# First input projection of a two-layer backbone: fed from x times the scale alone, with the reciprocal root applied where it leaves PSUM

## The chip, the core and the metric

The kernel runs on one core of one Trainium2 chip, in one launch. The metric is device time in microseconds (us), from the first to the last instruction of the core and what lies around them. TensorE is called PE, its weight loads PEld, VectorE DVE, ScalarE ACT, GpSimd POOL; SP is the engine that issues the transfers.

## The reference

Two layers work on 512 latent tokens (`x`) and 256 context tokens (`ctx`) of width 1024. Each layer has a token mixer and a gated ConvFFN. What the change touches is the head of the first layer:

```python
mod_lat = (silu_c @ w_ada[l] + b_ada[l])[:, None, :]      # six parts: sh1, sc1, gt1, sh2, sc2, gt2
h  = modulate(rms_norm(x, g_mix[l]), sh1, sc1)            # rms_norm(x) * (1 + sc1) + sh1
hc = modulate(rms_norm(ctx, g_mix[l]), csh1, csc1)
f_in, c_q, c_kv, k_rope_raw = split_in_proj(h @ w_in[l])
```

and the same projection of `hc`. `c_q` and `c_kv` are normalised again and projected to queries, keys and values; the rope part is rotated; `f_in` goes through a two-dimensional Fourier transform. Attention, an output projection and the ConvFFN follow; the second layer repeats all of it for the latent tokens.

## The kernel before

Activations lie transposed: 128 features on the partitions, tokens along the row. The 1024 features are eight tiles `x[0]` to `x[7]` of 128 x 768, latent tokens in columns 0 to 511 (`LAT`), context in 512 to 767 (`CTX`). Every large product is taken in three matmuls (`mm3`, L109): operands are split into a high part of reduced mantissa and a low remainder, and high x high (L112), high x low (L113) and low x high (L114) are accumulated. ACT makes the high part of a weight by a cast (L101), POOL or DVE subtracts for the low part (L107), PE multiplies. The input projection has seven strips of 128 outputs: kv, q0, q1, q2, the rotary key kr, and the Fourier strips f0 and f1.

The modulation vectors come from the matrix product `ada` (L151): a chunk is eight pieces of 256 KB of `w_ada`, eight narrow matmuls (L163; the trace holds two records of each, one per pass), a copy by ACT (L165), four transposes on PE (L171), and three short DVE instructions (L175, L176, L183) that leave scale and shift for two feature tiles. So chunks 0 to 3 serve tiles 0/1, 2/3, 4/5 and 6/7. The pieces lie in the buffers `q` and `k`, eight of each, so a third chunk waits until the first is used.

`program` (L738) writes the start. `begin` (L744) loads a segment, `norm_x` squares the eight tiles on ACT (L249), sums them on DVE (L254, L257), sums over partitions by a matmul with ones (L267) and forms the reciprocal root of the mean by Ln, Exp, Square and two DVE steps (L270 to L274); then every tile is multiplied by that root on DVE or POOL (L751). `affine` (L288) scales and shifts each tile: ACT writes the high part `H` (L296), DVE or POOL writes scaled x in place (L298), DVE the low part (L299). `feed` (L326) multiplies. The first three strips kv, q0, q1 are fed as tiles come: tiles 0 to 3 for the latent tokens, then for the context tokens, then tiles 4 to 7 for both. The fourth strip q2 follows, fed from complete `H`. A finished strip is copied out of PSUM by ACT in one pass (L355; f0 and f1 by L349 and L350); two PSUM buffers `big` of 1024 columns and four `sm` of 512 hold the accumulators.

After the projection, `lowrank_norm` (L382) normalises kv and the three q strips, `rot` (L397) rotates kr, and `attention` (L472) copies the rotated key into the four key tiles on POOL (L486).

The program text doesn't fix the order on each engine: a scheduler of the framework orders all instructions by its own estimate of when each can start. Each engine then works its list strictly in order and waits at every entry for its inputs. SP issues transfers in order, and at most eight are under way.

## Time and profile before

| what | us |
|---|---|
| median of 3 runs | 1633.55 |
| the runs | 1629.89, 1633.55, 1633.59 |
| span of the profiled execution | 1629.7 |
| PE busy in it | 1580.5 (97%) |
| DVE, ACT, POOL busy in it | 1091.3, 718.6, 361.8 |

The span is counted from the first to the last instruction. The page gives no time of the profiled execution beside it; the fastest run lies 0.2 us above the span and the median 3.9.

A stretch of the trace is read by three questions: was PE busy, at which granted clock, and what ended its idle time. Matmuls are pipelined and the ends in the records are modelled, so their spacing, from start to start, says more than their length.

### The profile page before, as it was taken

To read this page: it belongs to the slowest core of one execution; us is meant where nothing else is said; L and a number is where in the kernel's file an instruction comes from. 1 tells how busy PE (TensorE), PEld (TensorE's weight loads), DVE (VectorE), ACT (ScalarE), POOL (GpSimd) and SP (SyncE) were. 2 spreads that over 40 slices of the span, in tenths; PEclk is the share of its full clock that TensorE was granted. 3 is DMA by queue.
4 is the path that set the end of the run, shared out by engine and by line. 5 is a ranking of instruction groups with operands and counts; after the bars stand their busy time and mean duration, and the time that the engine had idled before them with its cause. 6 is when DMAs were issued, how large, how long until landed. Compare 5 with 4: busy or idle time off the path is not lost.

```text
span 1629.7 us, 24211 instructions
## 1 busy us (share of the span) xinstructions
PE 1580.5 (97%) x9093; PEld 1316.5 (81%) x9093; DVE 1091.3 (67%) x2117; ACT 718.6 (44%) x1374; POOL 361.8 (22%) x388
## 2 busy tenths in 40 slices
PE   4999999999999999999999999899999999999997
PEld 1768677768988888888888887777789888888887
DVE  5557566644788966988688568776657664664656
ACT  4355566543643313331234445565545442442443
POOL 3426265452000000000000124654742000000012
PEclk9999999999999999999999999999999999999999
DMA  9441200222423443445333242000324123233333
GB/s 338 140 161 58 79 19 32 91 78 91 140 81 118 144 130 104 147 126 169 99 123 110 87 136 66 28 25 7 116 71 143 49 88 103 98 94 101 99 96 116
DMA packets 71252, 167.13 MB, mean 103 GB/s; under 512 B 7776, under 2 KB 25184, under 8 KB 71136
## 3 DMA queue, kind: packets, MB, share of 16 engines
q1 hardware_dynamic: 71136, 165.60, 32.0%
q8 instruction: 71, 1.16, 0.3%
q14 instruction: 45, 0.37, 0.1%
HBM read 161.37 MB, written 4.19 MB: 102 GB/s over the span
## 4 chain that ended last, share of the span: by engine, by line
PE 88%; DVE 5%; ACT 3%; issue 1%; DMA 1%; POOL 1%; SPq 0%; DVEq 0%; POOLq 0%; ACTq 0%
PE sm L112 16%; PE sm L114 16%; PE sm L113 16%; PE big L112 10%; PE big L113 10%; PE big L114 10%; PE sm L574 6%; PE sm L565 4%; PE sm L163 1%; ACT p L546 1%; DVE st L544 1%; DVE x L751 1%; PE sm L267 1%; DVE wl L107 0%; DVE q L503 0%
## 5 line engine op out<-in xcount | busy, mean ns | idle before, releaser
L101 ACT CAST wh<-wr 128x512 fp32r<-128x512 f32 (+2 forms) x346 | 203.0, 591 | 392.3 <-PE sm L113 242.7
L107 DVE TENSOR_TENSOR wl<-wr,wh 128x512 fp32r<-128x512 f32 (+2 forms) x290 | 199.8, 691 | 175.5 <-ACT wh L101 164.4
L107 POOL TENSOR_TENSOR wl<-wr,wh 128x512 fp32r<-128x512 f32 (+2 forms) x74 | 87.8, 1192 | 974.4 <-ACT wh L101 974.3
L112 PE MATMUL big<-H,wh 128*128 128x512 f32 (+1 forms) x664 | 234.3, 356 | 7.6 <-ACT H L296 7.0
L113 PE MATMUL big<-H,wh 128*128 128x512 f32 (+1 forms) x664 | 236.4, 356 | 2.4 <-DVE H L299 1.4
L112 PE MATMUL sm<-H,wh 128*128 128x512 f32 (+1 forms) x688 | 236.5, 344 | 0.0
L113 PE MATMUL sm<-H,wh 128*128 128x512 f32 (+1 forms) x688 | 235.7, 343 | 0.0
L114 PE MATMUL sm<-H,wl 128*128 128x512 f32 (+1 forms) x688 | 235.4, 342 | 0.0
L114 PE MATMUL big<-H,wl 128*128 128x512 f32 (+1 forms) x664 | 233.8, 353 | 0.0
L112 PE MATMUL sm<-q,wh 128*128 128x512 f32 (+1 forms) x528 | 179.5, 341 | 0.0
L113 PE MATMUL sm<-k,wh 128*128 128x512 f32 (+1 forms) x528 | 179.1, 340 | 0.0
L114 PE MATMUL sm<-q,wl 128*128 128x512 f32 (+1 forms) x528 | 178.8, 339 | 0.0
L220 DVE SCALAR_TENSOR_TENSOR p<-p,p 128x768 f32<-128x768 f32 x224 | 153.7, 686 | 2.4
L112 PEld LDWEIGHTS big<-H,wh 128*128 128x128 f32 x664 | 125.8, 190 | 29.8 <-ACT H L296 9.4
L113 PEld LDWEIGHTS big<-H,wh 128*128 128x128 f32 x664 | 126.2, 190 | 25.6 <-issue 3.3
L112 PEld LDWEIGHTS sm<-H,wh 128*128 128x128 f32 x688 | 130.4, 190 | 17.2 <-issue 1.5
L113 PEld LDWEIGHTS sm<-H,wh 128*128 128x128 f32 x688 | 130.4, 190 | 15.2 <-issue 0.2
L114 PEld LDWEIGHTS sm<-H,wl 128*128 128x128 f32 x688 | 130.3, 189 | 15.1
L114 PEld LDWEIGHTS big<-H,wl 128*128 128x128 f32 x664 | 126.1, 190 | 18.9 <-issue 1.3
L548 POOL TENSOR_SCALAR p<-p,st 128x768 f32<-128x768 f32 (+1 forms) x120 | 98.9, 829 | 143.7 <-DVE st L547 114.6
L544 DVE TENSOR_REDUCE st<-big 128x1 f32<-128x768 f32 x96 | 90.9, 954 | 27.9 <-PE big L114 24.9
L112 PEld LDWEIGHTS sm<-q,wh 128*128 128x128 f32 x528 | 100.2, 190 | 11.4 <-issue 0.2
(225 smaller groups left out, 3184.2 us busy)
## 6 DMA issues: line engine op xcount, KB each, us to landing
wr<-in_w_up SPq DMA_DIRECT2D x88, 512.0 KB, 3.2
p<-in_w_ada_t SPq DMA_DIRECT2D x74, 384.0 KB, 3.4
wr<-in_w_down SPq DMA_DIRECT2D x32, 448.0 KB, 3.3
wr<-in_w_out SPq DMA_DIRECT2D x24, 512.0 KB, 3.3
wr<-in_w_down SPq DMA_DIRECT2D x24, 512.0 KB, 3.6
q<-in_w_ada SPq DMA_DIRECT2D x32, 256.0 KB, 4.9
k<-in_w_ada SPq DMA_DIRECT2D x32, 256.0 KB, 4.7
wr<-in_w_in SPq DMA_DIRECT2D x12, 512.0 KB, 4.7
```

Source lines behind the costliest of these rows:

```text
L101: nc.scalar.copy(out=h, in_=x)
L107: eng.tensor_tensor(out=l, in0=x, in1=f(h), op=ALU.subtract)
L112: mm(out, wh, xh, start=start, stop=False)
L113: mm(out, wh, xl, start=False, stop=False)
L114: mm(out, wl, xh, start=False, stop=stop)
L163: nc.tensor.matmul(acc[32 * g:32 * g + 32, :], self.sc[:, k, :], ws[k], start=k < 4, stop=k >= 4)
L220: dot = nc.vector.scalar_tensor_tensor(out=junk[:, :w.shape[-1]], in0=w, scalar=1.0, in1=hold["c"][s][q], op0=ALU.mult, op1=ALU.mult, accu ...
L267: nc.tensor.matmul(s, self.ones, acc, start=True, stop=True)
L544: nc.vector.tensor_reduce(out=st[:, 0:1], in_=b[:, :nk], axis=AX.X, op=ALU.max, negate=True)
L548: nc.gpsimd.tensor_scalar(out=e[:, :nk], in0=e[:, :nk], scalar1=st[:, 2:3], scalar2=1.0, op0=ALU.mult, op1=ALU.mult)
L565: nc.tensor.transpose(out=tp[:, i, :], in_=Pn[j][:, (i0 + i) * P:(i0 + i + 1) * P], identity=self.ident)
L574: nc.tensor.matmul(acc[64 * j:64 * j + 64], V[t0 + i][:, hd:hd + HD], PT[j][i // 3][:, i % 3, :], start=i == 0, stop=i == nt - 1)
```

## The change

The reciprocal root is one number per token, so it can be taken out of the product over features. In the first layer `H` is now x times the scale alone (`scaled`: one ACT and one DVE instruction per tile and segment), and the projected strip is multiplied by the root when it leaves PSUM (`finish`: on DVE). The shift times the weight is the same for all tokens of a segment: the eight pieces of the two shift vectors are split like activations (`shifts`) and stand as columns 768 and 769 of `H`, so the context matmuls are 258 wide; their result is copied out (128 x 2) and added as a bias, on ACT, in the squares and in a pass over each strip. `norm_x` no longer stands ahead of the projection.

The loads are reordered: chunk 0 first, then tiles 0 and 1, the weights of three strips, tiles 2 to 7, chunk 1, context, chunk 2, the weight of q2 and two more, chunk 3. `q1` joins the first strips from the start, its high parts made by ACT. A few instructions are pinned to their place in the program's order. The padded silu vector `sc` moves into the buffer that later holds the conv weights `dw`, whose load so comes after the last modulation chunk of the first layer. The second layer is unchanged.

```diff
@@ -33,8 +33,10 @@
+NB2 = NT + 2
+CTXB = (NL, NB2)
@@ -118,7 +123,7 @@
-        self.sc = cp.tile([P, KD, 32], F32, name="sc")
+        self.sc = self.sb.tile([P, KD, 32], F32, name="sc", tag="dw", bufs=1)
@@ -243,15 +248,22 @@
     def stat_begin(self, cnt):
         return {"acc": None, "n": 0, "cnt": cnt}
 
-    def sq_add(self, st, xk):
+    def sq_add(self, st, xk, bias=None, pin=False):
         nc = self.nc
         sq = self.t("p")[:, :xk.shape[-1]]
-        nc.scalar.activation(out=sq, in_=xk, func=AF.Square)
+        if bias is None:
+            op = nc.scalar.activation(out=sq, in_=xk, func=AF.Square)
+        else:
...
@@ -285,24 +297,32 @@
-    def affine(self, x, k0, k1, s, seg, H):
+    def scaled(self, x, k0, k1, s, seg, H, pin=False):
         nc = self.nc
         lo, hi = seg
         for k in range(k0, k1):
             h, l = H[k]
+            a = self.A1[0][:, k, s:s + 1]
+            ops = [nc.scalar.activation(out=h[:, lo:hi], in_=x[k][:, lo:hi], func=AF.Identity, scale=a),
+                   nc.vector.scalar_tensor_tensor(out=l[:, lo:hi], in0=x[k][:, lo:hi], scalar=a, in1=f(h)[:, lo:hi], op0=ALU.mult, op1=ALU.subtract)]
+            if pin:
+                for op in ops:
+                    self.tc.keep_in_program_order(op)
+
+    def shifts(self, k0, k1, H):
+        nc = self.nc
+        for k in range(k0, k1):
+            h, l = H[k]
             c = 4 * (k // 2) + 2 + k % 2
-            a, b = self.A1[0][:, k, s:s + 1], self.mod[0][:, c, s:s + 1]
-            xk = x[k][:, lo:hi]
-            nc.scalar.activation(out=h[:, lo:hi], in_=xk, func=AF.Identity, scale=a, bias=b)
-            eng = nc.vector if k % 2 == 0 else nc.gpsimd
-            eng.tensor_scalar(out=xk, in0=xk, scalar1=a, scalar2=b, op0=ALU.mult, op1=ALU.add)
-            nc.vector.tensor_tensor(out=l[:, lo:hi], in0=xk, in1=f(h)[:, lo:hi], op=ALU.subtract)
+            b = self.mod[0][:, c, :]
+            nc.scalar.copy(out=h[:, NT:NB2], in_=b)
+            nc.vector.tensor_tensor(out=l[:, NT:NB2], in0=b, in1=f(h)[:, NT:NB2], op=ALU.subtract)
 
...
@@ -314,7 +334,7 @@
-            segs = [LAT] if l == 1 and n[0] in "qf" else [LAT, CTX]
+            segs = [LAT, CTXB] if l == 0 else [LAT] if n[0] in "qf" else [LAT, CTX]
@@ -354,16 +376,39 @@
-                out["ckv"] = self.lowrank_norm([raws["kv"]], self.vec[l][:, V_GKV:V_GKV + 1], P, [LAT, CTX])[0]
+                out["ckv"] = self.lowrank_norm([raws["kv"]], self.vec[l][:, V_GKV:V_GKV + 1], P, [LAT, CTX], l == 0 and [self.wb["kv"]])[0]
-                out["cq"] = self.lowrank_norm([raws["q0"], raws["q1"], raws["q2"]], self.gq[l], QR, [LAT] if l == 1 else [LAT, CTX])
+                out["cq"] = self.lowrank_norm([raws["q0"], raws["q1"], raws["q2"]], self.gq[l], QR, [LAT] if l == 1 else [LAT, CTX], l == 0 and [self.wb["q0"], self.wb["q1"], self.wb["q2"]])
+
+    def finish(self, n, pieces, raws, U):
+        nc = self.nc
+        r = self.t("p")
+        wb = self.sb.tile([P, 4], F32, name=self.nm("st"), tag="st", bufs=6)
+        nc.scalar.copy(out=wb[:, 0:2], in_=pieces[1][0][:, NC:NC + 2])
+        for s, (a, lo, hi) in enumerate(pieces):
+            hi = min(hi, NT)
+            nc.vector.tensor_tensor(out=r[:, lo:hi], in0=a[:, :hi - lo], in1=self.rstd[s], op=ALU.mult)
+        if n == "kr":
+            for s, (a, lo, hi) in enumerate(pieces):
+                hi = min(hi, NT)
+                nc.scalar.activation(out=r[:, lo:hi], in_=r[:, lo:hi], func=AF.Identity, bias=wb[:, s:s + 1])
+        if n[0] != "f":
+            raws[n] = r
+            self.wb[n] = wb
+            return
+        h, lw = self.hl("v")
+        for s, (a, lo, hi) in enumerate(pieces):
+            hi = min(hi, NT)
+            nc.scalar.activation(out=h[:, lo:hi], in_=r[:, lo:hi], func=AF.Identity, bias=wb[:, s:s + 1])
+            nc.vector.scalar_tensor_tensor(out=lw[:, lo:hi], in0=r[:, lo:hi], scalar=wb[:, s:s + 1], in1=f(h)[:, lo:hi], op0=ALU.add, op1=ALU.subtract)
+        U.append((h, lw))
@@ -379,13 +424,16 @@
-    def lowrank_norm(self, raws, g, cnt, segs):
+    def lowrank_norm(self, raws, g, cnt, segs, wb=None):
         nc = self.nc
         outs = [self.hl("x") for _ in raws]
-        for lo, hi in segs:
+        for s, (lo, hi) in enumerate(segs):
             st = self.stat_begin(cnt)
-            for r in raws:
-                self.sq_add(st, r[:, lo:hi])
+            for i, r in enumerate(raws):
+                self.sq_add(st, r[:, lo:hi], wb and wb[i][:, s:s + 1])
+            if wb:
+                for i, r in enumerate(raws):
+                    nc.scalar.activation(out=r[:, lo:hi], in_=r[:, lo:hi], func=AF.Identity, bias=wb[i][:, s:s + 1])
             y = self.stat_end(st)
             for i, r in enumerate(raws):
                 h, l = outs[i]
@@ -741,41 +789,46 @@
 
-        def begin(s, seg, src):
+        self.rstd, self.wb = {}, {}
+
+        def load(seg, src, ks=range(KD)):
             lo, hi = seg
-            for k in range(KD):
+            for k in ks:
                 nc.sync.dma_start(out=x[k][:, lo:hi], in_=src[:, k, :])
-            rstd = self.norm_x(x, seg)
-            for k in range(KD):
-                eng = nc.gpsimd if k % 4 == 3 else nc.vector
-                eng.tensor_tensor(out=x[k][:, lo:hi], in0=x[k][:, lo:hi], in1=rstd, op=ALU.mult)
 
         self.ln_exp()
-        begin(0, LAT, A["xT"])
-        H = [self.hl("H") for _ in range(KD)]
         first = ("kv", "q0")
         runs = [self.ada(0, 0, "qkv")]
-        pre = {n: self.weight(A["w_in"][0, idx[n]], KD, leng="pool") for n in first}
+        load(LAT, A["xT"], range(2))
+        runs[0]()()
+        pre = {n: self.weight(A["w_in"][0, idx[n]], KD, leng="pool", pin=n == "kv") for n in first}
+        pre["q1"] = self.weight(A["w_in"][0, idx["q1"]], KD, leng="pool", tags=("v", "qs"))
+        load(LAT, A["xT"], range(2, KD))
+        H = [tuple(self.t("H", F32R, [P, NB2]) for _ in range(2)) for _ in range(KD)]
         runs.append(self.ada(0, 1, "qkv"))
         begun = self.group(first, 0)
+        begun.update(self.group(("q1",), 0))
         for i in range(2):
             ks = range(2 * i, 2 * i + 2)
-            runs[i]()()
-            self.affine(x, ks[0], ks[-1] + 1, 0, LAT, H)
+            if i:
+                runs[i]()()
+            self.scaled(x, ks[0], ks[-1] + 1, 0, LAT, H)
             self.feed(begun, pre, H, ks, [LAT])
-        pre["q1"] = self.weight(A["w_in"][0, idx["q1"]], KD, heng="pool", tags=("v", "qs"))
-        more = self.group(("q1",), 0)
-        self.feed(more, pre, H, range(4), [LAT])
-        begun.update(more)
-        begin(1, CTX, A["ctxT"])
-        self.affine(x, 0, 4, 1, CTX, H)
-        self.feed(begun, pre, H, range(4), [CTX])
+            if i == 0:
+                self.rstd[0] = self.norm_x(x, LAT)
+        load(CTX, A["ctxT"])
+        self.scaled(x, 0, 4, 1, CTX, H, True)
+        self.shifts(0, 4, H)
+        self.feed(begun, pre, H, range(4), [CTXB])
         runs = [self.ada(0, 2, "qkv"), self.ada(0, 3, "qkv")]
+        self.rstd[1] = self.norm_x(x, CTX)
         for i in range(2):
             ks = range(4 + 2 * i, 6 + 2 * i)
             runs[i]()()
-            for c, seg in enumerate((LAT, CTX)):
-                self.affine(x, ks[0], ks[-1] + 1, c, seg, H)
+            for k in ks:
+                for c, seg in enumerate((LAT, CTX)):
+                    self.scaled(x, k, k + 1, c, seg, H)
+            self.shifts(ks[0], ks[-1] + 1, H)
             self.feed(begun, pre, H, ks)
         self.late_consts()
         spill = None
```

How the change moves instructions is shown at three places. The first is PE where the latent half of the first strips meets the norm matmul and chunk 1. Before, the chunks follow one another (`sc` is the silu vector, `H` the scaled tiles, 214 and 215 the accumulators of kv and q0):

```order
L163 MATMUL sm_216<-k_176,sc 32x512
L171 MATMUL sm_227<-ident,v_225 128x128 x4
L163 MATMUL sm_253<-q_198,sc 32x512
L163 MATMUL sm_253<-k_200,sc 32x512
L163 MATMUL sm_253<-q_202,sc 32x512
L163 MATMUL sm_253<-k_204,sc 32x512
L163 MATMUL sm_253<-q_206,sc 32x512
L112 MATMUL big_214<-H_146,wh_180 128x512
L112 MATMUL big_215<-H_146,wh_190 128x512
L163 MATMUL sm_253<-k_208,sc 32x512
```

Now the last matmuls of tiles 0 and 1 (205 is q1's accumulator) stand first, then the norm matmul (`p` and `ones`), then chunk 1:

```order
L118 MATMUL sm_205<-H_174,v_157 128x512
L119 MATMUL sm_205<-H_173,qs_158 128x512
L279 MATMUL sm_252<-p_231,ones 128x512
L168 MATMUL sm_261<-q_187,sc 32x512
L168 MATMUL sm_261<-k_189,sc 32x512
L168 MATMUL sm_261<-q_191,sc 32x512
L168 MATMUL sm_261<-k_193,sc 32x512
L168 MATMUL sm_261<-q_195,sc 32x512
L168 MATMUL sm_261<-k_197,sc 32x512
L168 MATMUL sm_261<-q_199,sc 32x512
L168 MATMUL sm_261<-k_201,sc 32x512
L176 MATMUL sm_272<-ident,v_270 128x128 x4
```

The norm matmul, which was PE's first instruction, has moved behind the first tiles and ahead of chunk 1.

The second place is PE at the transposes of chunk 3. Before, they stand in front of tile 4's products (`H_155` is its low part):

```order
L112 MATMUL sm_300<-H_154,v_296 128x512
L112 MATMUL sm_301<-H_154,v_296 128x256
L171 MATMUL sm_520<-ident,v_518 128x128 x4
L113 MATMUL big_214<-H_155,wh_184 128x512
L114 MATMUL big_214<-H_154,wl_185 128x512
L112 MATMUL big_214<-H_154,wh_184 128x256
```

Now (`H_182` and `H_181` are tile 5's low and high part, `H_183` tile 6's high part):

```order
L119 MATMUL big_204<-H_181,wl_152 128x258
L118 MATMUL sm_206<-H_182,v_161 128x258
L119 MATMUL sm_206<-H_181,qs_162 128x258
L176 MATMUL sm_504<-ident,v_502 128x128 x4
L117 MATMUL big_203<-H_183,wh_141 128x512
L117 MATMUL big_204<-H_183,wh_151 128x512
L117 MATMUL sm_205<-H_183,v_161 128x512
```

The transposes have moved from ahead of the pair 4/5 to between that pair and the pair 6/7.

The third is DVE at the rotation of the key kr. Before, the shuffle and the rope multiplication (L400, L401; `p_919` is kr) stand among the steps of the query norm:

```order
L273 SCALAR_TENSOR_TENSOR p_803<-sm_800,p_803 128x256
L400 STREAM_SHUFFLE p_1113<-p_919 128x512
L274 SCALAR_TENSOR_TENSOR p_802<-p_803,p_802 128x256
L401 TENSOR_TENSOR p_1113<-p_1113,rope 128x512
L392 SCALAR_TENSOR_TENSOR p_585<-p_585,gq_75,p_802 128x256
L392 SCALAR_TENSOR_TENSOR p_635<-p_635,gq_75,p_802 128x256
L392 SCALAR_TENSOR_TENSOR p_724<-p_724,gq_75,p_802 128x256
L403 TENSOR_TENSOR p_919<-p_919,p_1113 128x512
```

Now they stand behind the new multiplications of the Fourier strips (L397; `p_254` and `p_419` are the roots of the two segments, `p_922` is kr):

```order
L442 TENSOR_TENSOR x_760<-p_627,x_759 128x256
L442 TENSOR_TENSOR x_762<-p_718,x_761 128x256
L397 TENSOR_TENSOR p_1023<-sm_963,p_254 128x512
L397 TENSOR_TENSOR p_1023<-sm_964,p_419 128x256
L397 TENSOR_TENSOR p_1111<-big_1052,p_254 128x512
L397 TENSOR_TENSOR p_1111<-big_1052,p_419 128x256
L448 STREAM_SHUFFLE p_1133<-p_922 128x512
L180 TENSOR_REDUCE mod_72<-sm_1034 128x8
L410 SCALAR_TENSOR_TENSOR v_1029<-p_1023,st_1024,v_1028 128x512
L410 SCALAR_TENSOR_TENSOR v_1029<-p_1023,st_1024,v_1028 128x256
L410 SCALAR_TENSOR_TENSOR v_1117<-p_1111,st_1112,v_1116 128x512
L449 TENSOR_TENSOR p_1133<-p_1133,rope 128x512
```

The shuffle of kr has moved behind f0 and f1.

## Rows read from the trace of the kernel before

**Rows 1.** The engine table of the profile: busy us, share of the span, instructions
```profile
span 1629.7 us, 24211 instructions
...
PE 1580.5 (97%) x9093; PEld 1316.5 (81%) x9093; DVE 1091.3 (67%) x2117; ACT 718.6 (44%) x1374; POOL 361.8 (22%) x388
```

**Rows 2.** Stretches: length, busy of PE, PEld, DVE, ACT, POOL, granted clock, DMA, GB/s
```profile
12.89:29.70 16.81, 9.92 (x32) 2.34 (x32) 11.73 (x12) 5.38 (x10) 10.07 (x6) 0.98 1.05 375
29.70:36.70 7.00, 7.00 (x15) 2.73 (x15) 4.09 (x6) 1.57 (x4) 2.74 (x3) 0.56 1.05 390
36.70:55.46 18.76, 16.74 (x107) 11.41 (x107) 12.64 (x32) 8.87 (x18) 6.28 (x7) 1.00 0.75 263
55.46:69.25 13.79, 13.46 (x81) 11.56 (x77) 7.21 (x17) 6.42 (x12) 6.35 (x11) 1.00 0.44 142
69.25:114.00 44.75, 44.75 (x259) 33.03 (x258) 25.22 (x47) 20.57 (x43) 10.33 (x17) 1.00 0.44 142
```

**Rows 3.** Waits of PE up to 69.25 us: total, times, longest
```profile
PE sm L267 <- DVE p L257: 12.9, 1, 12.9
PE big L112 <- ACT H L296: 7.0, 2, 6.0
```

**Rows 4.** Timeline of PE, start to fourth strip: start, length, instruction, idle before
```profile
12.89 2.08 PE L267 MATMUL sm<-p,ones 128*128 128x512 f32 x2 [12.89 <-DVE p L257]
...
29.70 1.22 PE L112 MATMUL big<-H,wh 128*128 128x512 f32 x2 [6.05 <-ACT H L296]
...
33.30 0.63 PE L114 MATMUL big<-H,wl 128*128 128x512 f32 x1
33.73 0.63 PE L113 MATMUL big<-H,wh 128*128 128x512 f32 x1
...
69.25 0.40 PE L112 MATMUL big<-H,wh 128*128 128x512 f32 x1
69.48 0.40 PE L113 MATMUL big<-H,wh 128*128 128x512 f32 x1
```

**Rows 5.** Timeline of the transfer queue SP: start, length, transfer issued
```profile
11.16 0.33 SPq L156 DMA_DIRECT2D k<-in_w_ada  x1
...
19.87 0.33 SPq L86 DMA_DIRECT2D wr<-in_w_in  x1
```

**Rows 6.** Timeline of all engines behind chunk 2, 50 to 56 us
```profile
53.08 0.60 PE L171 MATMUL sm<-ident,v 128*128 128x128 f32 x4
...
53.61 0.62 PE L163 MATMUL sm<-q,sc 128*32 128x512 f32 x1
...
54.34 1.30 ACT L296 ACTIVATE H<-x,mod,a 128x512 fp32r<-128x512 f32 x2 [5.61 <-DVE a L183]
...
55.46 0.73 PE L112 MATMUL big<-H,wh 128*128 128x512 f32 x2
```

**Rows 7.** Groups by line and shape, 0 to 140 us: busy, mean ns, idle before
```profile
L107 POOL TENSOR_TENSOR wl<-wr,wh 128x512 fp32r<-128x512 f32 x4 | 6.7, 1704 | 0.0
...
L296 ACT ACTIVATE H<-x,mod,a 128x512 fp32r<-128x512 f32 x8 | 6.3, 808 | 15.6 <-DVE a L183 15.6
...
L350 DVE TENSOR_TENSOR v<-sm,v 128x512 fp32r<-128x512 f32 x1 | 0.7, 691 | 1.5 <-ACT v L349 1.5
```

**Rows 8.** Instructions on the tiles x, 0 to 30 us: ns minimum, median, maximum
```profile
L249 ACT ACTIVATE p<-x x8: 612/630/631, 5.3 to 11.2; 128x512 f32<-128x512 f32 x8
...
L751 DVE TENSOR_TENSOR x<-x,p x6: 691/1746/1760, 18.4 to 25.7; 128x512 f32<-128x512 f32 x6
```

**Rows 9.** Timeline of POOL in the attention and in the ConvFFN
```profile
115.76 3.42 POOL L486 TENSOR_SCALAR k<-p 64x768 fp32r<-64x768 f32 x4 [7.13 <-ACT v L349]
...
129.70 3.97 POOL L107 TENSOR_TENSOR q<-wr,q 32x768 fp32r<-32x768 f32 x2
...
370.82 1.29 POOL L107 TENSOR_TENSOR wl<-wr,wh 128x512 fp32r<-128x512 f32 x1 [11.14 <-ACT wh L101]
```

**Rows 10.** Timeline of PE at the first scores
```profile
133.36 0.47 PE L112 MATMUL big<-k,q 128*128 128x512 f32 x1 [1.52 <-ACT q L502]
```

More of the change, by code (lines that the diff above doesn't have):

```diff
@@ L81, in sm, with weight @@
         return self.ps.tile([P, 512], F32, name=self.nm("sm"), tag="sm", bufs=4)
-    def weight(self, src, nk, m=P, heng="act", leng="dve", tags=("wh", "wl")):
+    def weight(self, src, nk, m=P, heng="act", leng="dve", tags=("wh", "wl"), pin=False):
         nc = self.nc
@@ L93, in weight @@
             pick = lambda e: e if isinstance(e, str) else e[i % len(e)]
-            self.split(wh, wl, raw[:, k0:k1, :], pick(heng), pick(leng))
+            op = self.split(wh, wl, raw[:, k0:k1, :], pick(heng), pick(leng))
+            if pin and i == 0:
+                self.tc.keep_in_program_order(op)
             parts.append((wh, wl))
@@ L100, in split @@
         if heng == "act":
-            nc.scalar.copy(out=h, in_=x)
+            op = nc.scalar.copy(out=h, in_=x)
         elif heng == "dve":
-            nc.vector.tensor_copy(out=h, in_=x)
+            op = nc.vector.tensor_copy(out=h, in_=x)
         else:
-            nc.gpsimd.tensor_scalar(out=h, in0=x, scalar1=1.0, scalar2=1.0, op0=ALU.mult, op1=ALU.mult)
+            op = nc.gpsimd.tensor_scalar(out=h, in0=x, scalar1=1.0, scalar2=1.0, op0=ALU.mult, op1=ALU.mult)
         eng = nc.vector if leng == "dve" else nc.gpsimd
         eng.tensor_tensor(out=l, in0=x, in1=f(h), op=ALU.subtract)
+        return op
     def mm3(self, out, w, x, start, stop):
@@ L244, in stat_begin @@
         return {"acc": None, "n": 0, "cnt": cnt}
-    def sq_add(self, st, xk):
+    def sq_add(self, st, xk, bias=None, pin=False):
         nc = self.nc
         sq = self.t("p")[:, :xk.shape[-1]]
-        nc.scalar.activation(out=sq, in_=xk, func=AF.Square)
+        if bias is None:
+            op = nc.scalar.activation(out=sq, in_=xk, func=AF.Square)
+        else:
+            op = nc.scalar.activation(out=sq, in_=xk, func=AF.Square, bias=bias)
+        if pin:
+            self.tc.keep_in_program_order(op)
         eps = EPS * st["cnt"] / P
@@ L253, in sq_add @@
         elif st["n"] == 1:
-            nc.vector.scalar_tensor_tensor(out=sq, in0=st["acc"], scalar=eps, in1=sq, op0=ALU.add, op1=ALU.add)
+            op = nc.vector.scalar_tensor_tensor(out=sq, in0=st["acc"], scalar=eps, in1=sq, op0=ALU.add, op1=ALU.add)
+            if pin:
+                self.tc.keep_in_program_order(op)
             st["acc"] = sq
@@ L345, in w_in @@
             for n in names:
-                if n[0] == "f":
+                if l == 0:
+                    self.finish(n, accs[n][0], raws, U)
+                elif n[0] == "f":
                     h, lw = self.hl("v")
```

6 lines of the change are left out of this document (4 added, 2 removed).

## The prediction

> **What bounds the kernel now.** I read the engine table first: TensorE (PE) is busy 97% of the span [rows 1], so time can only come from stretches in which it waits or runs slowly. The table of stretches says where those are. Between its first matmul at 12.89 us and the first matmul of the fourth projection strip at 69.25 [rows 4], 56.4 us pass. The work in it, at the fast spacing of 0.23 us for 512 columns [rows 4] and half of it for 256, is 72 matmuls of either width (16.6 + 8.6 us), four modulation chunks of 1.85 [rows 6], four times four transposes of 0.5 and two norm matmuls (1.3): about 36 us. [...] The list of waits names the holders: 12.9 us for VectorE's sum of squares, 7.0 for ACT's scaled x [rows 3]. From 55.46 on PE is full.
>
> What moves the end is therefore the instant at which PE reaches that fourth strip, plus what the changed copying out does afterwards. From PE's 740th instruction on, in the first layer's attention, PE's order is the same in both kernels, so a shift there reaches the end.
>
> **The start, step by step.** Transfers are a chain: the issue at 11.16 waits for the eighth 256 KB piece, the one at 19.87 for the 21st [rows 5], hence (19.87 - 11.16)/13 = 0.67 us per piece. In the new order the eighth piece ends modulation chunk 0 (11.2), x0 and x1 land by 12.5, the strips kv, q0, q1 by 13.8, 15.2, 16.5, the rest of x by 20.5, chunk 1 by 25.9, ctx by 28.6, chunk 2 by 34, and chunk 3, behind 1.1 MB of later weights, by 43.
>
> First projection matmul: 11.2, plus 1.0 for the last chunk matmul (half of 2.08 [rows 4]), 0.9 for ACT's copy and two handovers, 1.9 from the transposes to the end of the first scaled tile (53.08 to the middle of the pair at 54.34 [rows 6]), 0.2 because that tile took 0.81 in the early stretch [rows 7], 0.6 for the cast of kv that stands behind it: 15.8, against 29.70 [rows 4]. That is 14 us earlier, and it is not the gain.
>
> From there POOL sets the pace: three strips need six subtractions of low parts, 1.29 each alone [rows 9], 1.70 beside VectorE [rows 7], so the third strip's last is out at 15.8 + 6 x 1.6 = 25.4. [...] Next on PE, ahead of chunk 1, stands the norm matmul of x. Its last six squares stand on ACT behind the first scaled tile (15.2) and nine passes of 0.6 (casts, the second tile, two squares): they start at 20.7, land one every 0.63 [rows 8] and end at 24.5. VectorE's sums are late: while POOL subtracts, a 512-wide add takes 1.75 instead of 0.69 (the median and minimum of one line, five beside POOL and one after it [rows 8]). Of the last six sums two fall under that and a third by half: 21.35 + 2 x 1.75 + 1.15 + 3 x 0.69 = 28.1. PE then waits 2.7 us.
>
> Fast, norm and chunk 1 take 0.85 + 1.85 [rows 6], to 30.8; then 2.85 of copy, transposes and VectorE before the next scaled tile: 33.6. Chunk pair 1 and the context columns of four tiles are 18 x 0.235 + 36 x 0.12 = 8.6: 42.2, or up to 44.2 if PE restarts slowly after that pause (five microseconds at half rate cost 2 to 2.5). Then norm 0.4, chunk 2 1.85, its copy 0.9 (transposes stand right behind it), transposes 0.5, chunk 3 1.85 (landed at 43, needed at 46), two tiles 6.2, transposes to first scaled tile 1.9 uncovered (the order puts chunk 3's transposes behind the first pair, where before they stood ahead of it), two tiles 6.2: 19.8. **Fourth strip at 62.0 to 64.0, instead of 69.25: 5.3 to 7.3 gained, middle 6.3.**
>
> The removed multiplications by the root (12 on VectorE, 4 on POOL) and the 16 affine passes lie in this stretch and are contained in it; the two extra columns in 168 context matmuls are 336 columns, 0.15 us.
>
> **What is added behind it.** Each of seven strips now leaves PSUM by two VectorE multiplications, 0.69 for 512 [rows 7] and some 0.4 for 256, instead of one ACT copy: 7.7 us more on VectorE between the fourth strip and the attention. VectorE is busy 25 of the 45 us after 69.25 [rows 2], so most is covered. Two places are not. PE's fourth strip needs kv's accumulator back: kv ends only 0.5 us earlier now, and 0.43 to 1.2 of multiplication follow: 0.2 to 0.8 lost. And the rotary key's rotation stands on VectorE behind the Fourier strips' multiplications; before, it stood ahead of them, and POOL copied the finished key from 115.76 on [rows 9]. Counted in the old kernel's times I get 114.0 for the first Fourier multiplications, 115.3 for the second, shuffle 116.0, four passes and the rope multiply to 119.3, the sum 120.3, ACT's split behind the key heads 122.1, POOL's copies to 125.6, its two subtractions for q until 134.7 instead of 133.7 [rows 9]. PE already waits 1.52 there [rows 10], so this comes through: 1.0 to 1.3. Lower end 0 if the four scores in front cover it. Together 1.6 (0.2 to 2.1).
>
> The conv vector's load now waits for the last modulation matmul, and a load of w_q stands behind it on the queue; that weight is needed some 15 us later, so it costs nothing, and a few microseconds only if that distance were gone.
>
> **Sum:** -6.3 + 1.6 = -4.7 us. The profiled span is 1629.7 [rows 1]; its own execution lies between that and the median, 0.2 to 3.9 above it. Taken off the median of 1633.55: **1628.8 us**, 0.29% less. What a measurement of this kernel can tell is about 0.3%, 4.9 us, so the forecast sits just inside "no change".
>
> **Rivals.**
> 1. *The slow clock stays.* PE rose to the full clock only after seven busy microseconds [rows 2]. In the new order its matmuls from 15.8 come in pieces between POOL's results. If it never rises before the pause at 25.4, norm takes 2.0 and chunk 1 3.5, the next tile comes at 36.5 and the pairs after it start slowly (10.9): fourth strip at 67.2, gain 2.1 less 1.6, 1633.0. Against it: 18.9 to 22.8 is dense. [...]
> 2. *The sums are not stretched.* Should VectorE and POOL pass each other with 0.69 and 1.29 each, the norm matmul starts at 25.4, chunk 1 ends at 28.0, and the gain grows by 2.7: 1626.1. For it: the pairs of rows 8 are in-place products, not sums.
> 3. *Slower.* The finishing work finds no cover: kr, both Fourier strips and the query norm want VectorE in the same 15 us, in which it already runs without a gap. If all 7.7 us and the later key come through PE and the start is that of rival 1: -2.1 + 7.7 + 1.2 = +6.8, 1640.3. It decides as soon as more than 7 us of the added work stands ahead of something that PE waits for. Against it: at most three strips finish there (3.3 us).
> 4. *The change does not do what it says:* chunk 3, issued later than before, arrives behind its need and holds the last two pairs. Landing at 43 it is 3 us early; it would have to slip past 51 to undo the gain, 1633.5.
>
> **How the numbers follow.** Forecast 0.46, rival 1 0.25 (its clock is the least certain step), rival 2 0.15, rival 3 0.11, rival 4 0.03. The forecast's own span is 62.0 to 64.0 and 0.2 to 2.1: from -7.1 to -3.2, 1626.4 to 1630.4, so about half of it lies beyond 4.9. Faster: 0.23 + 0.15 + 0.03 for a mixed start = 0.41; slower 0.11; the rest, 0.48, same. The range holds forecast and rivals 1, 2 and 4 with their bounds: 1624.5 to 1634.5.
>
> **What would show it.** First projection matmul near 16; the norm matmul of x near 28 behind slow VectorE sums; spacing 0.23 from some 24 us on; a pause of 2 to 3 us behind chunk 1; the fourth strip at 62 to 64; POOL's key copies about 7 us after the point of the old ones, counted from the fourth strip. A fourth strip before 60 or after 67, or more than 3 us of new waits between it and the attention, makes the forecast wrong.

## The result and the profile after

| | median us | runs | span of the profiled execution |
|---|---|---|---|
| before | 1631.97 (1629.89 to 1634.38) | 6 | 1629.7 |
| after | 1641.40 (1639.31 to 1641.53) | 6 | 1637.7 |

The ratio is 1.0054, with an interval of 1.0041 to 1.0067: the changed kernel is slower by about 8.8 us, 6.7 to 10.9. The forecast was 1628.8 within 1624.5 to 1634.5, so both the time and the sign were wrong. (It was taken off 1633.55, the median of three runs; with six the median before is 1631.97.)

The engine table of the changed kernel already holds the larger half of the answer:

```profile
span 1637.7 us, 24230 instructions
...
PE 1589.0 (97%) x9093; PEld 1315.0 (80%) x9093; DVE 1086.3 (66%) x2118; ACT 721.7 (44%) x1396; POOL 350.6 (21%) x376
```

PE executes as many matmuls as before, 9093, and is busy 8.5 us longer with them [rows 1]. That isn't a wait. To see where it arises, the same PE instruction was paired in the two timelines at several places, first in the kernel after:

```profile
67.42 0.47 PE L117 MATMUL big<-H,wh 128*128 128x512 f32 x1 [0.92 <-POOL wh L422]
...
188.71 0.41 PE L613 MATMUL sm<-ident,p 128*128 128x128 f32 x2 [0.26 <-ACT p L594]
...
352.51 0.30 PE L613 MATMUL sm<-ident,p 128*128 128x128 f32 x1 [0.30 <-POOL q L109]
...
987.29 0.51 PE L118 MATMUL big<-H,wh 128*128 128x512 f32 x1 [0.59 <-DVE H L298]
...
1171.43 0.50 PE L117 MATMUL big<-k,q 96*128 96x512 f32 x1 [0.28 <-ACT p L594]
...
1628.32 0.48 PE L279 MATMUL sm<-p,ones 128*128 128x256 f32 x1 [1.48 <-DVE p L269]
```

and their partners before, behind the fourth strip at 69.25 [rows 4]:

```profile
188.54 0.52 PE L565 MATMUL sm<-ident,p 128*128 128x128 f32 x3 [0.26 <-ACT p L546]
...
352.78 0.30 PE L565 MATMUL sm<-ident,p 128*128 128x128 f32 x1 [0.30 <-POOL q L105]
...
984.44 0.50 PE L113 MATMUL big<-H,wh 128*128 128x512 f32 x1 [0.60 <-DVE H L286]
...
1168.47 0.50 PE L112 MATMUL big<-k,q 96*128 96x512 f32 x1 [0.28 <-ACT p L546]
...
1620.29 0.48 PE L267 MATMUL sm<-p,ones 128*128 128x256 f32 x1 [1.49 <-DVE p L257]
```

After minus before is -1.83 at the fourth strip, +0.17 at 188.7, -0.27 at 352.5. So the part of the program that the change was about nets nothing. Then the distance grows where the change has no line: +2.85 at 987, +2.96 at 1171, +8.03 at 1628. The waits named at the three late places are as long as before, to 0.01 us. What grew are the matmuls on `H`. In the second layer there is a run of 336 of them, 512 columns wide, without a gap; two lines of the view of tile `H` there (number of matmuls; duration in ns: minimum, median, maximum; then first and last start in us), before:

```profile
L112 PE MATMUL big<-H,wh x64: 389/389/389, 1381.7 to 1457.2; 128*128 128x512 f32 x64
...
L114 PE MATMUL big<-H,wl x64: 389/389/389, 1382.2 to 1457.7; 128*128 128x512 f32 x64
```

and after:

```profile
L117 PE MATMUL big<-H,wh x64: 388/394/400, 1386.2 to 1463.4; 128*128 128x512 f32 x64
...
L119 PE MATMUL big<-H,wl x64: 391/395/399, 1386.6 to 1463.9; 128*128 128x512 f32 x64
```

Before, all 64 records of a line are equal; after, they scatter, and the whole run takes 77.72 us from first to last start (1386.16 to 1463.88) where it took 75.93 (1381.75 to 1457.68). Divided by 335, that is a spacing, from start to start, of 226.7 ns before and 232.0 after. From 1260 us on there are 960 of them in three such runs (288, 336 and 336): 960 x 5.3 ns = 5.1 us, which is the 5.07 that the distance grows from 1171 to 1628. Nothing in these lines was edited. What the edit changed, and what the experiments below test, is the address of the data: a tile `H` is 770 columns wide, and its buffer 3104 bytes from the next, where 768 columns gave 3072. All later users of these buffers inherit that.

The start of the changed kernel, on PE:

```profile
14.54 0.50 PE L117 MATMUL big<-H,wh 128*128 128x512 f32 x1 [1.94 <-ACT wh L105]
...
26.91 2.08 PE L279 MATMUL sm<-p,ones 128*128 128x512 f32 x2 [3.44 <-DVE p L269]
28.91 1.06 PE L168 MATMUL sm<-q,sc 128*32 128x512 f32 x1
...
31.49 1.06 PE L168 MATMUL sm<-k,sc 128*32 128x512 f32 x1
...
35.42 0.72 PE L117 MATMUL big<-H,wh 128*128 128x512 f32 x2 [1.43 <-ACT H L306]
...
45.71 0.60 PE L279 MATMUL sm<-p,ones 128*128 128x256 f32 x2
...
129.08 0.55 PE L117 MATMUL sm<-v,v 128*128 128x256 f32 x1 [3.86 <-DVE k L551]
```

and its stretches (columns as in rows 2; the second to fourth overlap others):

```profile
15.00:23.50 8.50, 6.10 (x18) 3.79 (x17) 7.28 (x6) 6.97 (x15) 8.50 (x6) 0.80 1.05 389
19.40:26.10 6.70, 2.34 (x9) 1.29 (x8) 6.24 (x5) 2.57 (x5) 4.51 (x3) 1.00 1.06 377
26.20:32.90 6.70, 5.65 (x18) 1.10 (x18) 2.04 (x3) 2.06 (x4) 0.00 (x0) 0.50 0.99 342
23.50:36.00 12.50, 6.88 (x25) 2.00 (x25) 5.70 (x11) 3.98 (x8) 0.41 (x1) 0.73 1.03 358
36.00:46.00 10.00, 10.00 (x55) 8.61 (x53) 5.58 (x16) 4.13 (x13) 0.79 (x2) 0.83 0.77 282
...
129.00:132.20 3.20, 3.12 (x14) 3.11 (x15) 1.55 (x4) 0.77 (x2) 0.32 (x1) 0.54 0.27 80
```

POOL is busy throughout the first of these, as forecast. But modulation chunk 1, which I had counted at the fast clock, comes with records of 1.06 us. The clock had risen: it is granted in full from 19.4 to 26.1. It fell to the lower level while PE waited for the norm's sums, and stayed there (0.50) for the norm matmul and the whole chunk; over 23.5 to 36 that averages 0.73.

### The profile page after: what moved, and what is told of

It is laid out like the page before. It is cut to its first block, busy times and chain, and to the rows that moved or that the text cites. A ratio compares the mean times of both kernels' runs of the same rounds, so it can differ in the third digit from the quotient of the medians.

```text
span 1637.7 us, 24230 instructions
## 1 busy us (share of the span) xinstructions
PE 1589.0 (97%) x9093; PEld 1315.0 (80%) x9093; DVE 1086.3 (66%) x2118; ACT 721.7 (44%) x1396; POOL 350.6 (21%) x376
## 4 chain that ended last, share of the span: by engine, by line
PE 87%; DVE 5%; ACT 3%; issue 2%; POOL 2%; DMA 1%; SPq 0%; DVEq 0%; POOLq 0%; ACTq 0%
PE sm L117 16%; PE sm L119 15%; PE sm L118 15%; PE big L117 10%; PE big L118 10%; PE big L119 9%; PE sm L622 6%; PE sm L613 4%; PE sm L168 2%; ACT p L594 1%; DVE st L592 1%; DVE p L269 1%; PE sm L279 1%; DMA wr<-in_w_q 0%; POOL wl L111 0%
## 5 line engine op out<-in xcount | busy, mean ns | idle before, releaser
L117 PE MATMUL big<-H,wh 128*128 128x512 f32 (+2 forms) x664 | 236.2, 358 | 6.3 <-ACT H L306 2.9
L118 PE MATMUL big<-H,wh 128*128 128x512 f32 (+2 forms) x664 | 237.6, 358 | 1.0 <-DVE H L298 0.9
L117 PE MATMUL sm<-H,wh 128*128 128x512 f32 (+2 forms) x688 | 237.5, 345 | 0.0
L119 PE MATMUL sm<-H,wl 128*128 128x512 f32 (+2 forms) x688 | 237.1, 345 | 0.0
L119 PE MATMUL big<-H,wl 128*128 128x512 f32 (+2 forms) x664 | 236.2, 356 | 0.6 <-POOL wl L111 0.6
L118 PE MATMUL sm<-H,wh 128*128 128x512 f32 (+2 forms) x688 | 236.1, 343 | 0.0
```

The source lines that it names most:

```text
L117: mm(out, wh, xh, start=start, stop=False)
L118: mm(out, wh, xl, start=False, stop=False)
L119: mm(out, wl, xh, start=False, stop=stop)
```

## The experiments

Two questions: is the address of `H` the cause of the growing distance, and what do the start and the later finish cost without it? The kernels of products only, and three others (norm late, kr first on the narrow version, split norm), were run once each: their traces are read, not their times.

**The width alone, in the kernel before.**

```diff
-        return self.sb.tile(shape or [P, NT], ...)
+        return self.sb.tile(shape or [P, NT + 2 if tag == "H" else NT], ...)
...
-        self.sc = cp.tile([P, KD, 32], F32, name="sc")
+        self.sc = self.sb.tile([P, KD, 32], F32, name="sc", tag="dw", bufs=1)
```

> The kernel before, with the same order of instructions on PE, DVE, ACT and POOL, and one thing changed: each of the 16 H tiles is allocated 770 columns wide instead of 768, as in the changed kernel, so that they lie 3104 bytes apart instead of 3072. (To make room the silu vector lies in the conv buffer; one load of 90 KB moves on the queue.) The two extra columns are never read. Theory A, the distance between the H tiles is what makes the products with H slower: in the stretch of 336 products before the last layer norm the spacing goes from 226.7 ns to about 232, and the time grows by 8 to 10 us, to 1640 to 1642 (ratio 1.005 to 1.006). Theory B, the lost 8 us come from where the other buffers lie in the changed kernel (weights ahead of H, other order of the pool): the spacing stays at 227 and the time within 0.1% of before. Theory C, it is the finishing work and what follows from it: no change either.

Measured: 1640.89 against 1631.82, ratio 1.0050 (1.0035 to 1.0066): 8.2 us, nearly all of the loss, from the width alone (`sc` only makes room for it, and PE, DVE, ACT and POOL keep their order). The spacing is 232.0 ns, and the view of tile `H` is that of the changed kernel:

```profile
L112 PE MATMUL big<-H,wh x64: 388/394/400, 1388.2 to 1465.5; 128*128 128x512 f32 x64
...
L114 PE MATMUL big<-H,wl x64: 391/395/399, 1388.7 to 1465.9; 128*128 128x512 f32 x64
```

**The change without the width** (called the narrow version below). The shift columns are left out, so the shift is missing from the result, and another column is copied out in their place; the loads, the late root and the finishing work stay.

```diff
-NB2 = NT + 2
+NB2 = NT
...
-        for k in range(k0, k1):
+        for k in range(0):
...
-        nc.scalar.copy(out=wb[:, 0:2], in_=pieces[1][0][:, NC:NC + 2])
+        nc.scalar.copy(out=wb[:, 0:2], in_=pieces[1][0][:, 0:2])
```

> The changed kernel without the two shift columns: H tiles 768 wide again, 3072 bytes apart, context products 256 wide, and the bias copied out of PSUM is another column (the shift is left out of the first layer's result). All else, the order of the loads, the finishing on DVE, the place of the pool's buffers, stays. Theory A: spacing of the last layer's 336 products back to 226.7 ns, 8.4 us less than the changed kernel, about 1632 to 1633, equal to before within 0.1%, because the start and the finishing together leave the trace 0.3 us ahead at 338 us. Theory B (place of the other buffers): stays at 1640 to 1641. Theory C (finishing work): stays as well.

Measured: 1634.10 against 1631.82, ratio 1.0016 (1.0007 to 1.0025). Spacing 226.7; at 338 us PE stands 0.09 us ahead of the kernel before. Here `sc` lies in its new buffer too, so that move is not what costs. Both kernels together say that the loss is the width, and that the rest of the change gains nothing either: 2.6 us slower (1.1 to 4.1), where equal to before was expected.

**Which distance, and whether neighbours matter.** A kernel of products only: nine stretches of 192, alike but for the distance of the moving tiles; once alone, once with DVE, ACT and POOL working beside it.

> Only products: nine stretches of 192 matmuls of 512 columns (high x high, high x low, low x high over eight pairs of tiles, as the kernel has them), which differ in the distance of the 16 moving tiles alone: 3072, 3104, 3136, 3200, 3328, 3584, 4096, 3088 and 3080 bytes. No other engine works beside them; the reference is not computed. Theory A in its simple form (the distance itself): 227 ns at 3072 and 4096, 232 at 3104; which multiple is enough (64, 128, 256, 512, 1024) is read from the other stretches. Rival A2, the distance matters only while other engines use the memory: 227 in all nine.

> The same nine stretches with DVE (two-input products of 768 columns), ACT (copies of 768) and, in the first part, POOL (copies of 768) at work beside them, on other tiles; the reference is not computed. If the distance alone decides, the nine spacings are those of the run without neighbours; if it is contention with other engines, they differ here and not there.

Mean spacing of the stretch, alone (the first one counted from where the clock is granted in full, at 27.4 us):

```
distance, bytes   3072   3104   3136   3200   3328   3584   4096   3088   3080
spacing, ns      226.7  231.5  231.2  233.3  226.8  226.7  226.7  231.4  232.2
```

Beside the other engines each number is the same within 0.1 ns. The view of the moving tile in the kernel alone, for distances 3104, 3200 and 3328:

```profile
L53 PE MATMUL sb<-M,wh x64: 391/396/399, 68.0 to 111.8; 128*128 128x512 f32 x64
...
L53 PE MATMUL sd<-M,wh x64: 393/395/396, 156.9 to 201.0; 128*128 128x512 f32 x64
...
L53 PE MATMUL se<-M,wh x64: 389/389/390, 201.7 to 244.5; 128*128 128x512 f32 x64
```

The fast distances (226.7 to 226.8 ns) are those of the nine that are multiples of 256 bytes. It is no contention with the other engines: in the second kernel DVE, ACT and POOL are each busy for 94% or more of the 399 us of products (267, 462 and 267 instructions), and no stretch changes by more than 0.1 ns.

**Distance, or place against the weights?** Twelve stretches with the tiles and the weights shifted against each other, the first to let the clock rise.

> Only products again, 192 of 512 columns to a stretch, high x high, high x low, low x high over eight pairs of moving tiles; the reference is not computed. Moving tiles 3072 bytes apart, weights 512 (stretch a); all moving tiles 32, 64, 128 bytes further (b, c, d); all weights 32 and 128 bytes further (e, f); weights 544 bytes apart (g); moving tiles 3104 bytes apart, but with all high tiles first and then all low ones, so that a pair is congruent to 256 bytes and only the step to the next pair is not (h); the low tiles 128 bytes off their high ones (i); every second pair 128 bytes off (j); one tile for all (k). Theory A1, it is the step from one moving tile to the next that must be a multiple of 256 bytes: a to g and k at 227 ns, h and j between 227 and 231 (one step in three is off), i above 231. Theory A2, it is how the moving tile lies to the weights: b to g slow (230 to 236), k at 227.

```
all tiles and weights alike modulo 256          226.7
one moving tile for all                         226.9
all moving tiles +32 / +64 / +128               233.3 / 228.9 / 232.4
all weight blocks +32 / +128                    233.3 / 233.4
weight blocks 544 bytes apart                   231.5
low tiles +128 / every second pair +128         233.3 / 232.2
tiles 3104 apart, all high ones ahead of low    232.4
```

```profile
L53 PE MATMUL sa<-M,V x64: 389/389/389, 66.7 to 109.6; 128*128 128x512 f32 x64
...
L53 PE MATMUL sb<-M,V x64: 393/394/397, 110.3 to 154.4; 128*128 128x512 f32 x64
...
L53 PE MATMUL se<-M,V x64: 395/396/396, 243.7 to 287.8; 128*128 128x512 f32 x64
```

In `sb` and `se` the distance between moving tiles is 3072, as in the fast `sa`; only their place against the weights differs. So it is not the step from tile to tile: in these stretches 226.7 to 226.9 ns came only where moving tile and weight block lie alike modulo 256 bytes, and all of them. The addresses of the built kernels agree: in the kernel before, every `H` buffer and every weight buffer lies at 96 modulo 256; in the changed kernel the weights still do, and the sixteen `H` buffers take all eight multiples of 32 in turn. In the first 3328-byte version below all of them lie at 0, and its spacing is 226.7 as well, so it is the place against the weights that counts, not a start at a multiple of 256. Shifting the weights alone by 32 bytes costs 6.6 ns a product (233.3 against 226.7). Why this is so no run shows. How large the loss is for a given difference stays open: +64 costs 2.2 ns and +32 costs 6.6, and in mixed stretches a product whose own tile and weights lie alike is slow as well (with only the low tiles shifted, the median record of high x high is 397 ns, against 389 in `sa`).

**The whole change at 3328 bytes.** Two versions. The first makes room by one buffer `p` less (and one each of `st` and `part`, and a few small tiles put together):

```diff
-    SLOTS = {..., "p": 9, ...}
+    SLOTS = {..., "p": 8, ...}
...
-        H = [tuple(self.t("H", F32R, [P, NB2]) ...
+        H = [tuple(self.t("H", F32R, [P, 832]) ...
```

> The changed kernel whole, shifts included, with its H tiles 3328 bytes apart (13 x 256) instead of 3104. The room for it comes from the p buffers, eight instead of nine, and a few small tiles put together. Theory A: the spacing in the last layer's stretch of 336 products goes from 232 to 227 ns and the time from 1641.4 to about 1633 to 1634, that of the run without shift columns. Rival: only 3072 as in the kernel before is fast in the whole program, or the missing p buffer costs as much as the distance gave: 1638 or more.

Measured: 1639.83, ratio 1.0043 (1.0030 to 1.0057). The spacing is 226.7 and from 1171 us on the distance grows by no more than 0.3 us, but PE stands 6.9 us behind the narrow version from 338 to 1000 us. At the fourth strip it is 2.3 us ahead of it; then it waits 3.16 us at 102 us for a sum on DVE (0.78 in the narrow version), and it is 3 us behind at 135 us and 6 at 190. The second version shows that this comes from the room that was made; that it is the missing `p` buffer was not tested by itself. Both theories had a part, and the time alone would have hidden that. The second version takes the room from memory reserved for transfers that this kernel does not use:

```diff
-    nc = bacc.Bacc("TRN2", ..., num_devices=1)
+    nc = bacc.Bacc("TRN2", ..., num_devices=1, dynamic_dma_scratch_size=12288)
...
-        H = [tuple(self.t("H", F32R, [P, NB2]) ...
+        H = [tuple(self.t("H", F32R, [P, 832]) ...
```

> The changed kernel whole, with the same order of instructions on all five queues, and one thing changed: its H tiles lie 3328 bytes apart (13 x 256) instead of 3104. The room comes from the framework's scratch for descriptors at the bottom of the memory, 12 KB instead of 16, which this kernel does not use. Theory A2 (a product is slower by 2 to 10 ns when its moving tile does not lie at the same place within 256 bytes as its weights): 232 to 227 ns in the last layer's 336 products, and 8 us less than the changed kernel: 1633 to 1634.5, with before at 1632. Rival: 1637 or more, as with the missing p buffer.

Measured: 1634.42 against 1631.25, ratio 1.0011 (1.0001 to 1.0020), with the instructions of every engine in the order of the changed kernel. This is the 3328-byte version from here on. The view of `H` is back to that of before:

```profile
L117 PE MATMUL big<-H,wh x64: 389/389/389, 1384.7 to 1460.2; 128*128 128x512 f32 x64
...
L119 PE MATMUL big<-H,wl x64: 389/389/389, 1385.1 to 1460.6; 128*128 128x512 f32 x64
```

So 62 columns more than needed save about 7 us. The rest of the change still gains nothing.

**What holds the start.** First the whole norm of x one pair of tiles later (on the narrow version):

```diff
-            if i == 0:
+            if i == 1:
                 self.rstd[0] = self.norm_x(x, LAT)
```

> The run without shift columns (768 wide, shift left out), with one step of the start moved: the norm of x is written behind the second pair of tiles instead of ahead of modulation chunk 1, so that its matmul no longer stands on PE in front of that chunk. Theory S (the start is lost at this matmul, which waits for the sums, and in the low clock behind it): chunk 1, all landed by about 25.5 us, is done by 27 to 28 instead of 32.7, its scaled tile is multiplied at 29.5 to 31 instead of 35.5, and the fourth strip starts 4 to 6 us earlier than in the run without shift columns (67.6), at 62 to 64. Rival T (the transfers or ACT and DVE hold the next pair, or the clock falls all the same): less than 1.5 us of it reaches the fourth strip.

Chunk 1 came 6.2 us earlier and the next pair at 29.43, but the fourth strip only at 69.79: the 62 to 64 expected were missed. The squares had moved with the norm, and ACT's scaled context tiles stand behind them:

```profile
36.67 1.10 PE L279 MATMUL sm<-p,ones 128*128 128x512 f32 x2 [1.16 <-DVE p L269]
...
40.18 0.58 PE L117 MATMUL big<-H,wh 128*128 128x256 f32 x2 [2.41 <-ACT H L306]
```

So only the sum over partitions should move, one matmul, with squares and sums left where they are (on the 3328-byte version; the scheduler also moves some transfers from 29 us on):

```diff
             if i == 0:
-                self.rstd[0] = self.norm_x(x, LAT)
+                st = self.stat_begin(D)
+                for k in range(KD):
+                    self.sq_add(st, x[k][:, :NL], None, k < 2)
...
         self.feed(begun, pre, H, range(4), [CTXB])
+        self.rstd[0] = self.stat_end(st)
```

> The kernel of the first run of this call with the norm of x divided: squares and sums stay where they are, only the sum over partitions and the root move behind the second pair of tiles. Unlike the earlier attempt the squares aren't moved on ACT. Theory S: modulation chunk 1 follows the first strips without the wait of 3.4 us, its tiles are multiplied at 29.5 to 31 instead of 35.4, the context follows without the wait that the earlier attempt had at 40, and the fourth strip starts 3.5 to 5.5 us earlier, at 62 to 64. Rival T (the low clock and the later chunks' transfers give it back): at 66 or later.

```profile
23.50 0.62 PE L168 MATMUL sm<-q,sc 128*32 128x512 f32 x1
...
25.25 1.04 PE L168 MATMUL sm<-k,sc 128*32 128x512 f32 x2
...
29.06 0.73 PE L117 MATMUL big<-H,wh 128*128 128x512 f32 x2 [1.44 <-ACT H L306]
...
63.66 0.47 PE L117 MATMUL big<-H,wh 128*128 128x512 f32 x1 [0.92 <-POOL wh L422]
```

```profile
23.50:36.00 12.50, 10.39 (x56) 6.60 (x56) 7.70 (x17) 6.53 (x16) 0.52 (x1) 1.00 1.03 345
```

Without the wait of 3.44 us the clock stays granted (1.00 from 23.5 to 36, where the changed kernel and the 3328-byte version had 0.73), chunk 1 ends at 26.3, and the fourth strip starts at 63.66 instead of 67.42 (67.74 in the 3328-byte version). From 338 to 1000 us PE stands 3.7 us ahead of the kernel before; from 1050 us on, 1.1 to 1.3.

**What holds the attention.** The rotation of kr directly behind its strip (on the narrow version):

```diff
+            if names[0] == "kr" and l == 0:
+                self.rot(raws["kr"])
...
-        self.rot(kr)
+        if l:
+            self.rot(kr)
```

> The run without shift columns (768 wide, shift left out), with the rotation of the rotary key written directly behind its strip, ahead of the two Fourier strips, so that on VectorE its shuffle no longer stands behind their multiplications. Theory K (this is what PE's wait of 3.9 us at 129 us is made of): the wait falls under 1 us, and at 135 us the kernel stands 3 to 4 us earlier against the run without shift columns. Of that some may be lost again by 190 us, since both kernels stood level there. Rival L (the wait is for VectorE's backlog as a whole, not for the order): it stays within 1 us of 3.9.

Waits of PE from 100 to 190 us (total, times, longest), the narrow version:

```profile
PE sm L117 <- DVE k L551: 3.8, 1, 3.8
```

and with kr first:

```profile
PE sm L117 <- ACT wh L105: 1.6, 1, 1.6
PE big L117 <- ACT q L552: 1.5, 1, 1.5
PE sm L119 <- POOL wl L111: 0.9, 1, 0.9
```

The wait is gone and PE is 4.5 us ahead at 130 us, but shorter waits give most of that back (the first of these was 0.9 in the narrow version, the second 0.2). From 190 to 1000 us it is 1.2 to 1.5 us ahead; but 0.7 of that stood at the fourth strip already, where the edit has no part yet, so 0.5 to 0.8 us are kept. The same on the 3328-byte version:

> The kernel of the run before it, and the rotation of the rotary key written behind its strip. The run with the narrow tiles gained 4.5 us at 130 us by it and kept 1.3 to 1.5 us from 190 us on: here the same, the wait of 3.9 us on the low part of k gone, 1.2 to 1.5 us less than the run before it in the trace, 1632 to 1633. If it keeps the whole 4.5, 1629; if nothing, 1633.5.

Measured: 1632.44, ratio 1.0005 (0.9996 to 1.0014). The median is 2.0 us under that of the 3328-byte version, but the two intervals overlap and the means differ by 0.8; in the traces PE is 0.7 us ahead from 190 to 1000 us, 0.2 of it from the fourth strip. So a gain is likely and not shown by the time.

**All three repairs.** 3328 bytes, kr first and the split norm:

> Both edits on the kernel with the H tiles 3328 bytes apart. If the two gains stand beside each other and are kept: 4 to 5 us from the start and 1.3 from the key, 1627 to 1629, under the kernel before (1632) by 0.2%. If what comes early only waits later, as when the kernels stood level at 190 us: 1632 to 1633.

Measured: 1630.22 (1628.47 to 1631.97, 11 runs) against 1631.25, ratio 0.9992 (0.9983 to 1.0000). By the ratios it is about 10 us under the changed kernel, 3.1 under the 3328-byte version, and 1.3 us under the one before (0 to 2.8), which just touches no change; 1627 to 1629 had been expected. PE's fourth strip is at 64.70, and PE is 3.3 us ahead at 338 us. From 1050 us on only some 1.0 of this is left: in the trace 2.2 us are lost at the start of the second layer's attention, where PE waits 2.1 us for ACT and 1.8 for DVE and the kernel before waits 1.2 and not at all. The width-alone and the 3328-byte kernels lose some 1.7 us there by the same two waits, though their order is that of the kernel before and of the changed kernel, which have no such loss. What decides that is not settled.

## Why the prediction was wrong

**The step that failed first** is "the two extra columns in 168 context matmuls are 336 columns, 0.15 us". I counted the columns that PE reads and not the tile that holds them. The width of these tiles sets the distance of sixteen buffers, and those carry the moving operand of the largest products of both layers. That term, put at 0.15 us, was measured by itself at 8.2 (ratio 1.0050). I also wrote that from the 740th PE instruction on the order is the same, "so a shift there reaches the end". The order is the same, but I took equal order for equal time, and of the 3.3 us by which the kernel with all repairs is ahead at 338 us only about 1.0 reaches the end. The second layer has no changed line, yet its `H` buffers moved, and more than half of the loss is there (5.07 us). No rival had this. Rival 3 came near the right time, 1640.3, by luck: its way was DVE's finishing work, and between the fourth strip and 352 us the change lost 1.6 us, not 8.9.

**The second step** is "Fast, norm and chunk 1 take 0.85 + 1.85". They took from 26.91 to 32.55, 5.6 us. The numbers are those of rival 1, which I gave 0.25: norm 2.08 (its 2.0), chunk 1 3.6 (its 3.5), the fourth strip at 67.42 (its 67.2). Its condition is not what happened: it had the clock never rise before the pause, and the clock was granted in full from 19.4 to 26.1, as the argument against that rival said. It fell in the wait, which was larger than I had it, 3.44 instead of 2.7; that fall, ahead of the norm matmul, was in no sum. With the wait the granted clock is 0.50 from 26.2 to 32.9, without it 1.00 from 23.5 to 36.

The rest, step by step:

| step | forecast | measured |
|---|---|---|
| first projection matmul | 15.8 | 14.54 |
| POOL's last low part out | 25.4 | 23.91 |
| norm matmul of x starts | 28.1 | 26.91 |
| chunk 1 done | 30.8 | 32.55 |
| next pair | 33.6 | 35.42 |
| pair and context columns done | 42.2 to 44.2 | 45.71 |
| fourth strip | 62.0 to 64.0 | 67.42 |
| kv's accumulator, wait at the fourth strip | 0.2 to 0.8 | 0.92 |
| key copies later, against the fourth strip | 7 | 9.1 |
| net loss between there and 352 us | 1.6 (0.2 to 2.1) | 1.6 |

The steps up to the norm matmul held to 1.5 us, with the right engine at each. The slow sums are there (three of the last six take 1.58 to 1.69 us while POOL works, three 0.69), so rival 2 falls: the wait behind them is what took the clock. From the chunk's end to the pair, 2.87 us were measured and 2.85 forecast. The five microseconds at half rate behind that pause, which make the upper end of 62.0 to 64.0, were my estimate and no run shows them: the pair and the context columns took 45.71 - 35.42 = 10.3 us instead of 8.6, at a mean granted clock of 0.83. Behind the context columns I counted 19.8 us to the fourth strip; it took 67.42 - 45.71 = 21.7, of which 0.92 is the wait for kv's accumulator, costed apart (the row names POOL, which had long been done; DVE's multiplications of kv, from 66.25 us on, free it). The last 1.0 us I have not split.

**The finish** had the right size by an incomplete path. The key was late as said. POOL's copies, at 123.02, then ran beside the rope product of the queries' rotation on DVE (L449 at 125.13):

```profile
122.55 0.96 DVE L111 TENSOR_TENSOR p<-p,p 128x768 fp32r<-128x768 f32 x1 [0.82 <-ACT p L105]
...
125.13 3.07 DVE L449 TENSOR_TENSOR p<-p,rope 128x512 f32<-128x512 f32 x1
128.24 1.03 DVE L551 TENSOR_TENSOR k<-sm,k 64x512 fp32r<-64x512 f32 x2
```

```profile
123.02 3.68 POOL L534 TENSOR_SCALAR k<-p 64x768 fp32r<-64x768 f32 x4 [3.08 <-issue]
```

That product takes 3.07 us; in the kernel before, where POOL's copies were done by then, it took 0.69:

```profile
124.17 0.69 DVE L401 TENSOR_TENSOR p<-p,rope 128x512 f32<-128x512 f32 x1
```

That POOL's work stretches it is read from the overlap and was not tested by itself. The key head behind it (L551) holds a PSUM buffer, and PE waits 3.86 us for that at 129.08; with kr first the wait is gone. I had looked for the wait at the scores, where the 1.52 [rows 10] shrank to 0.19 instead. PE is 4.5 us behind there, but only 0.17 at 188.7: the kernel before loses time in the same place, with its own wait and a clock of 0.69 behind it:

```profile
133.00:138.00 5.00, 4.61 (x21) 4.10 (x22) 4.05 (x8) 2.88 (x7) 0.67 (x1) 0.69 0.20 57
```

That I have not followed wait by wait, and a net loss of just the forecast 1.6 us is in part luck. Two of the prediction's own signs of being wrong were there: a fourth strip after 67 us, and more than 3 us of new waits (0.92 and 3.86). Rival 4 falls: between 46 and 67.5 us PE waits for no transfer, so chunk 3 held nobody.

So without the width the change costs 1.8 us (0.2 to 3.3, the 3328-byte version) instead of gaining 4.7: 4.5 to 4.8 of the 6.5 us between are the start (1.8 gained in the changed kernel and 1.5 in that version, instead of 6.3). The finish was as forecast in the changed kernel; in the 3328-byte version 1.5 us more are lost to the clock after the wait (last section).

## What to carry to other kernels

When a change alters a tile's width, write down the address of every buffer of that pool before and after, and look at the spacing of untouched matmuls on it; equal order is not equal time (here 8.2 us). The quickest sign is PE's busy time with an unchanged count of instructions (here 1589.0 us against 1580.5, with 9093). When work is put ahead of a busy engine's chain, price the wait it makes together with the clock after it (here 3.44 us, and then a granted clock of 0.50 from 26.2 to 32.9), and move only the instruction that waits, not what feeds it (here the fourth strip came at 63.66 us, and at 69.79 with the squares moved too).

## What the hardware showed

- A 512-column product takes 226.7 to 226.9 ns where all moving tiles and weight blocks lie alike modulo 256 bytes, and 228.9 to 233.4 in every other arrangement tried. With DVE, ACT and POOL at work beside it, each of the nine distances gave the same within 0.1 ns. Over the whole kernel the wider tiles cost 0.5% (8.2 us).
- After the wait of 3.86 us the granted clock was 0.54 in 129.0 to 132.2 and 1.00 from 132.2 to 138.0 (512-column spacing 0.23 us). In the 3328-byte version, with the same order and a wait of 3.80, it was still 0.53 until 135.2 and the scores began 1.5 us later, though PE had come only 0.16 us later to the end of the wait. Why it rises later there stays open (the 3328-byte version):

```profile
129.00:132.20 3.20, 2.96 (x13) 2.99 (x14) 1.54 (x5) 0.60 (x2) 0.49 (x1) 0.50 0.30 92
132.20:135.20 3.00, 3.00 (x9) 2.32 (x9) 2.89 (x5) 1.31 (x4) 2.14 (x3) 0.53 0.07 10
```
